# A hybrid decoder layer's norms over the model width: operands in PSUM, transposes in pairs, half of the chunks scaled on VectorE

## The chip, the cores and the metric

The kernel runs on one NeuronCore of a Trainium2 chip. The metric is the device time of one execution in microseconds (us); lower is better. The engines are named as in the profile: PE is TensorE (matrix multiply; PEld is its weight load), DVE is VectorE, ACT is ScalarE, POOL is GpSimd, SP is SyncE, whose queue issues the loads. SBUF is the on-chip memory that all engines read, PSUM the accumulation memory that PE writes and that DVE and ACT read and write.

## The reference

One decoder layer over 256 tokens of width 2048, all in float32: a SwiGLU feed-forward half step, a mixer (attention beside a convolution), and a second half step, each followed by a layer norm over the model width.

```python
x = layer_norm(ALPHA * x + 0.5 * swiglu_ffn(x, w_gate1, w_up1, w_down1), ln1_g, ln1_b)
u = x @ w_in + b_in
mixed = concat([attention(q, k, v, sinks), conv_group(conv_in)]) @ w_out + b_out
x = layer_norm(ALPHA * x + mixed, ln2_g, ln2_b)
x = layer_norm(ALPHA * x + 0.5 * swiglu_ffn(x, w_gate2, w_up2, w_down2), ln3_g, ln3_b)
```

Here `layer_norm(x, g, b)` is `(x - mean) * rsqrt(var + eps) * g + b` along the 2048 columns. The first two norms (`ln1`, `ln2`) are the ones that the change touches.

## The kernel before

**Products.** Each float32 product is made of three products of split operands: an operand is a high part (rounded to a reduced format, by a copy on ACT) and a low part (the rest, by a subtraction on DVE or POOL). A weight unit of 128 x 1024 is thus loaded, copied to `hi` by ACT (L126) and subtracted to `lo` by DVE or, for the units listed in `pooled`, by POOL (L128). `POOL_FIRST` lists the units just behind each of the two norms whose subtraction POOL does: 0, 1, 2 and 4. Units are called u0, u1, ... below, counted from the norm.

**Two token blocks.** The 256 tokens are two blocks b = 0 and 1 of 128 partitions. The product ahead of a norm (`tokens_by`) sums into one PSUM tile `acc` per block and per 512 columns. Its last six weight units are held back for block 1 (`SKEW`): PE ends block 0 first, and while it does the six held steps of block 1 (six matmuls each), the other engines turn block 0 into the operand of the next product. When a block's last sum is done, DVE evacuates it (L265), takes the statistics (L268, L320) and the inverse root (`rsqrt`, one column wide, L278 to L288). All of this stands in DVE's queue in the order in which the code emits it.

**From tokens to features** (`norm_to_features`, once per block and norm). The 2048 columns are four chunks c = 0 to 3 of 512. DVE makes `z = (x - mean) * r` for all four (L325). PE turns each chunk by four transposes into a PSUM tile `tp` (L302); a tile holds two chunks, and there are two such tiles (`psA`, tag `gu`). ACT applies gain and bias, which lie along partitions after the transpose, in four pieces of 128 x 128, from PSUM into `z` in SBUF (L310), then copies the chunk to the high half of `xcat` (L311); DVE subtracts for the low half (L312).

**The order.** Nothing is scheduled by the compiler: each engine runs its instructions in the order of emission. `Steps` counts steps; `LN_AT` is a table of (step after the call, chunk, action), action 0 being the transposes, 1 the scaling, 2 the low half. Before the change block 0's transposes of chunk 0 come after the fourth held step, and those of chunks 1, 2 and 3 after the fifth. The next product (`token_group`, tile `grp`) starts after the sixth; its step t needs chunk t // 2 of `xcat` and unit ut, six steps for block 0, then six for block 1, then the last two for both. Block 1's transposes stand between block 0's steps of this product.

**Waits.** An instruction that needs another engine's result waits on a semaphore; one that needs an earlier result of its own engine does so too. The order listings below show these waits by engine (`Activation_49` is ACT, `DVE_49` DVE, `PE_49` PE, `DMAHW` a load).

Of the kernel before, what the change touches and what calls it, by code (L numbers as in the profile page):

```python
# [9 lines left out]
F32 = mybir.dt.float32  # L10
# [3 lines left out]
AF = mybir.ActivationFunctionType  # L14
ALU = mybir.AluOpType
# [3 lines left out]
P = 128  # L19
# [24 lines left out]
CAP = 4.0  # L44
CONV_AT = (1, 3, 1)
HB = 5
POOL_FIRST = (0, 1, 2, 4)
POOL_SPAN = (20, 84)
POOL_SHARE = (4, 7)
ZB = 5  # L50

LN_AT = ((5, 0, 0), (5, 0, 1), (6, 1, 0), (6, 2, 0), (6, 1, 1), (6, 3, 0), (6, 0, 2), (6, 2, 1), (7, 3, 1), (7, 0, 2), (7, 0, 2), (8, 0, 2))
ATT = (1, 1, 2, 2, 4, 6, 7)
ENGINES = {getattr(mybir.EngineType, e) for e in ("PE", "DVE", "Activation", "Pool", "SP")}

# [125 lines left out]
def hybrid_layer(  # L181
# [3 lines left out]
    nc = tc.nc  # L185
# [7 lines left out]
    psC = ctx.enter_context(tc.tile_pool(name="psC", bufs=1, space=PSUM))  # L193
# [25 lines left out]
    for n in (first, second):  # L219
        pooled |= {n + i for i in POOL_FIRST}  # L220
    st = Steps(nc, wpool, items, sources, pooled, xT, xcat)
# [9 lines left out]
    for lo_, base, mult, step in ((0, 0, 1, -1), (P, -1, -1, 1), (2 * P, 0, 1, -1)):  # L231
        nc.gpsimd.affine_select(
            out=mask[:, lo_ : lo_ + P], in_=mask[:, lo_ : lo_ + P], compare_op=ALU.is_ge,
            fill=NEG, base=base, pattern=[[step, P]], channel_multiplier=mult,
        )
    bias = const.tile([P, 26], F32, name="bias")
# [4 lines left out]
    xt = act.tile([P, 2, D], F32, name="xt")  # L241
# [31 lines left out]
    def rsqrt(var, y, between=()):  # L273

        v = small.tile([P, 1], F32, tag="rs_v", name="rs_v")
        w = small.tile([P, 1], F32, tag="rs_w", name="rs_w")
        t = small.tile([P, 1], F32, tag="rs_t", name="rs_t")
        nc.vector.tensor_scalar(out=v, in0=var, scalar1=EPS, scalar2=None, op0=ALU.add)  # L278
        nc.vector.tensor_scalar(
            out=y.bitcast(I32), in0=v.bitcast(I32), scalar1=-0.5, scalar2=RSQRT_SEED,  # L280
            op0=ALU.mult, op1=ALU.add,
        )
        nc.vector.tensor_scalar(out=w, in0=v, scalar1=-0.5, scalar2=None, op0=ALU.mult)
        for _ in range(3):
            if between:
                between.pop(0)()
            nc.vector.tensor_scalar(out=t, in0=y, scalar1=y, scalar2=w, op0=ALU.mult, op1=ALU.mult)
            nc.vector.tensor_scalar(out=y, in0=t, scalar1=1.5, scalar2=y, op0=ALU.add, op1=ALU.mult)  # L288
# [3 lines left out]
    def norm_to_features(b, stats, par, gcol, xc):  # L292

        mv, r = par[:, b, 0:2], par[:, b, 2:3]
        zs, tps = [], []

        def turn(c):
            if c % 2 == 0:
                tps.append(psA.tile([P, 2, 4, P], F32, tag="gu", name=f"tp{b}_{c}"))
            tp = tps[c // 2][:, c % 2]  # L300
            for k in range(4):
                nc.tensor.transpose(tp[:, k], zs[c][:, k * P : (k + 1) * P], ident)  # L302

        def scale(c):
            tp = tps[c // 2][:, c % 2]
            k4, cols = slice(4 * c, 4 * c + 4), slice(b * P, (b + 1) * P)
            full = zs[c].rearrange("p (k n) -> p k n", k=4)
            for k in range(4):
                g, be = (lnp[:, gcol + n, 4 * c + k : 4 * c + k + 1] for n in range(2))
                nc.scalar.activation(full[:, k], tp[:, k], AF.Identity, scale=g, bias=be)  # L310
            nc.scalar.copy(xc[:, k4, 0, cols], full)  # L311
            waiting.append(lambda: nc.vector.tensor_tensor(  # L312
                out=xc[:, k4, 1, cols], in0=full, in1=xc[:, k4, 0, cols].bitcast(F32), op=ALU.subtract
            ))

        def settle(most=9):
            for _ in range(min(most, len(waiting))):
                waiting.pop(0)()

        nc.vector.bn_aggr(out=mv, in_=stats[b].rearrange("p c s -> p (c s)"))  # L320
        rsqrt(mv[:, 1:2], r, waiting)
        settle()
        for c in range(NC_):
            z = act.tile([P, 512], F32, tag="z", name=f"z{b}_{c}", bufs=ZB)
            nc.vector.tensor_scalar(  # L325
                out=z, in0=xt[:, b, c * 512 : (c + 1) * 512], scalar1=mv[:, 0:1], scalar2=r,
                op0=ALU.subtract, op1=ALU.mult,
            )
            zs.append(z)
        for n, c, what in LN_AT:  # L330
            st.at(n, lambda c=c, what=what: (turn(c) if what == 0 else scale(c) if what == 1 else settle(1)))

    def residuals(par, row, more, eng, start, every):

# [210 lines left out]
    x1 = act.tile([P, KT, 2, S], F32R, tag="xcat", name="xcat1")  # L545
    par1, par2, par3 = params("par1"), params("par2"), params("par3")
    ffn(xcat, "1", 0, begun1, lambda pool: None, lambda b, s: norm_to_features(b, s, par1, 0, x1))


# [355 lines left out]
```

## Time and profile before

| | before |
|---|---|
| device time, three runs | 1789.01, 1789.95, 1790.3 us (median 1789.95) |
| the profiled execution | 1786.97 us |
| its span, first to last instruction | 1785.2 us |
| mean granted TensorE clock | 0.997 |
| DVE busy | 1058.7 us (59%) |
| ACT busy | 837.8 us (47%) |
| POOL busy | 142.2 us (8%) |
| bytes read from HBM | 332.86 MB, 188 GB/s over the span |

The profile is of one execution, whose own time is 1786.97 us; the span leaves out 1.8 us ahead of the first and behind the last instruction. The times of its rows are microseconds from the start of the span. A row of the timeline gives start, length, engine, line, operation, output <- input, their sizes, a count of merged instructions, and in brackets how long the engine had been idle and what ended the wait. The first norm lies at 731 to 770 us, the second at 1024 to 1063 us.

### The profile page before, as it was taken

Reading aid. Unit: us, or ns where it says so; the run is one execution under the profiler, and the core shown is the slowest. Engines: PE = TensorE matmul, PEld = TensorE weight load, DVE = VectorE, ACT = ScalarE, POOL = GpSimd, SP = SyncE. Lnnn points to the kernel's source line nnn. Section 1 sums busy time; section 2 is a strip of 40 time slices with the busy share of each in tenths; the row PEclk is TensorE's granted clock in tenths of the full one; section 3 lists DMA queues with packets and bytes.
Section 4 is the critical chain, followed back from the end, with each engine's and each line's share of the span. In section 5 each row is a group of like instructions: output and inputs, shape, how many; then the busy total and the mean of one; then the engine's idle time right before and its main releaser. Section 6 shows DMA issues by size and latency. Waiting matters only on the chain.

```text
span 1785.2 us, 23510 instructions
## 1 busy us (share of the span) xinstructions
PE 1750.2 (98%) x9550; PEld 1510.2 (85%) x9550; DVE 1058.7 (59%) x1386; ACT 837.8 (47%) x1145; POOL 142.2 (8%) x82
## 2 busy tenths in 40 slices
PE   8999999999999999999998999999999999999997
PEld 7888888888888888789997778888888888888885
DVE  6555555445555555658889676855544455555546
ACT  6544444334444443575653574544443334444431
POOL 0000000000000000205654420000000000000000
PEclk9999999999999999999999999999999999999999
DMA  9655555554555555445534445555555555555651
GB/s 334 236 189 189 189 189 189 193 200 175 188 189 189 189 210 190 148 163 179 179 142 165 165 165 200 215 189 189 187 201 189 193 200 189 188 188 189 223 209 48
DMA packets 52092, 336.48 MB, mean 188 GB/s; under 512 B 6288, under 2 KB 6416, under 8 KB 13072
## 3 DMA queue, kind: packets, MB, share of 16 engines
q1 hardware_dynamic: 51984, 334.98, 51.6%
q8 instruction: 75, 1.23, 0.3%
q14 instruction: 33, 0.27, 0.0%
HBM read 332.86 MB, written 2.10 MB: 188 GB/s over the span
## 4 chain that ended last, share of the span: by engine, by line
PE 95%; DVE 3%; ACT 1%; DMA 0%; issue 0%; SPq 0%; DVEq 0%
PE gu L491 35%; PE gu L497 18%; PE acc L384 10%; PE acc L386 10%; PE acc L385 10%; PE in_c L384 2%; PE in_c L385 2%; PE in_c L386 2%; PE grp L386 1%; PE grp L385 1%; PE grp L384 1%; PE in_q L384 1%; DVE z L325 1%; PE in_q L385 1%; PE in_q L386 1%; DVE conv L649 0%
## 5 line engine op out<-in xcount | busy, mean ns | idle before, releaser
L128 DVE TENSOR_TENSOR lo<-raw,hi 128x1024 fp32r<-128x1024 f32 (+1 forms) x569 | 701.9, 1240 | 234.7 <-ACT hi L126 233.6
L126 ACT CAST hi<-raw 128x1024 fp32r<-128x1024 f32 (+1 forms) x614 | 640.5, 1048 | 348.8 <-PE acc L386 319.6
L491 PE MATMUL gu<-xcat,hi 128*128 128x512 f32 x2688 | 673.1, 392 | 0.0
L491 PEld LDWEIGHTS gu<-xcat,hi 128*128 128x128 f32 x2688 | 483.7, 189 | 86.6
L497 PEld LDWEIGHTS gu<-xcat,lo 128*128 128x128 f32 x2688 | 366.7, 190 | 26.2
L497 PE MATMUL gu<-xcat,lo 128*128 128x256 f32 x2688 | 374.8, 282 | 0.0
L511 DVE TENSOR_TENSOR both<-gu,corr 128x512 f32<-128x512 f32 x84 | 58.1, 692 | 382.4 <-ACT corr L510 382.4
L384 PE MATMUL acc<-hi,hh 128*128 128x512 f32 x704 | 274.1, 389 | 0.0
L385 PE MATMUL acc<-lo,hh 128*128 128x512 f32 x704 | 273.9, 389 | 0.0
L386 PE MATMUL acc<-hi,hl 128*128 128x512 f32 x704 | 273.9, 389 | 0.0
L510 ACT COPY corr<-gu 128x512 f32<-128x512 f32 x84 | 49.2, 586 | 415.6 <-PE gu L497 415.6
L128 POOL TENSOR_TENSOR lo<-raw,hi 128x1024 fp32r<-128x1024 f32 x45 | 112.2, 2501 | 810.7 <-ACT hi L126 810.6
L386 PEld LDWEIGHTS acc<-hi,hl 128*128 128x128 f32 x704 | 132.2, 188 | 27.4
L384 PEld LDWEIGHTS acc<-hi,hh 128*128 128x128 f32 x704 | 132.2, 188 | 27.3
L385 PEld LDWEIGHTS acc<-lo,hh 128*128 128x128 f32 x704 | 132.2, 188 | 27.1
L649 DVE SCALAR_TENSOR_TENSOR conv<-hc,cw_sb,conv 128x256 f32<-128x256 f32 x232 | 93.5, 481 | 3.3 <-ACT conv L645 3.3
L384 PE MATMUL in_c<-xcat,hi 128*128 128x256 f32 x256 | 73.9, 289 | 0.0
L386 PE MATMUL in_c<-xcat,lo 128*128 128x256 f32 x256 | 72.4, 283 | 0.0
L385 PE MATMUL in_c<-xcat,hi 128*128 128x256 f32 x256 | 72.4, 283 | 0.0
L265 DVE SCALAR_TENSOR_TENSOR xt<-acc,xt 128x512 f32<-128x512 f32 x48 | 32.9, 689 | 55.9 <-PE acc L386 55.9
L384 PE MATMUL acc<-hi,mh 128*128 128x512 f32 x128 | 51.1, 399 | 7.0 <-DVE xt L265 4.6
L384 PEld LDWEIGHTS in_c<-xcat,hi 128*128 128x128 f32 x256 | 49.0, 191 | 2.4 <-issue 2.3
(125 smaller groups left out, 1121.9 us busy)
## 6 DMA issues: line engine op xcount, KB each, us to landing
raw<-in_wu SPq DMA_DIRECT2D x168, 1024.0 KB, 4.8
raw<-in_wd SPq DMA_DIRECT2D x88, 1024.0 KB, 4.7
raw<-in_win SPq DMA_DIRECT2D x26, 1024.0 KB, 4.8
raw<-in_wout SPq DMA_DIRECT2D x16, 1024.0 KB, 4.7
raw<-in_wt SPq DMA_DIRECT2D x4, 1024.0 KB, 4.7
raw<-in_wt SPq DMA_DIRECT2D x6, 512.0 KB, 6.5
xt<-in_x SPq DMA_DIRECT2D x2, 1024.0 KB, 7.7
rg<-in_rows SPq DMA_DIRECT2D x8, 256.0 KB, 5.1
```

Source lines behind the costliest of these rows:

```text
L126: nc.scalar.copy(hi, raw)
L128: eng.tensor_tensor(out=lo, in0=raw, in1=hi.bitcast(F32), op=ALU.subtract)
L265: nc.vector.scalar_tensor_tensor(out=y, in0=ps, scalar=factor, in1=y, op0=ALU.mult, op1=ALU.add)
L325: nc.vector.tensor_scalar(out=z, in0=xt[:, b, c * 512 : (c + 1) * 512], scalar1=mv[:, 0:1], scalar2=r, op0=ALU.subtract, op1=ALU.mult,)
L384: nc.tensor.matmul(ps, s_hi, m_hi, start=start, stop=False)
L385: nc.tensor.matmul(ps, s_hi, m_lo, start=False, stop=False)
L386: nc.tensor.matmul(ps, s_lo, m_hi, start=False, stop=stop)
L491: nc.tensor.matmul(gu[:, m, :], hi[:, q * P : (q + 1) * P], xc[:, k].rearrange("p a n -> p (a n)"), start=k == 0, stop=False,)
L497: nc.tensor.matmul(gu[:, m, S:], lo[:, q * P : (q + 1) * P], xc[:, k, 0, :], start=False, stop=k == KT - 1,)
L510: nc.scalar.copy(corr, gu[:, :, S:])
L511: nc.vector.tensor_tensor(out=both, in0=gu[:, :, :S], in1=corr, op=ALU.add)
L649: nc.vector.scalar_tensor_tensor(out=acc if k < CK - 1 else cv[:, i], in0=hc[:, k : k + S], scalar=cw_sb[:, i, k : k + 1], in1=acc, op0=AL ...
```

## The change

Five things change, all at the two norms:

- `z` is made by an instruction with two tensor inputs (L339 of the changed kernel): the second is `r`, copied to one column of a PSUM tile `rp` (L336) and read for every column.
- Gain and bias are applied in place in the PSUM tile `tp`: chunks 0 and 1 by ACT (L314), chunks 2 and 3 by DVE (L316), each in four pieces of 128 x 128.
- The high half is copied and the low half subtracted from `tp` in PSUM (L323, L324), no longer from `z` in SBUF.
- In `LN_AT` the transposes come in pairs: chunks 0 and 1 after the third held step (step 4 of the table), 2 and 3 after the fourth. Action 2 is now the high half and 3 the low half.
- POOL takes the subtraction of u3 as well.

```diff
-POOL_FIRST = (0, 1, 2, 4)
+POOL_FIRST = (0, 1, 2, 3, 4)
-LN_AT = ((5, 0, 0), (5, 0, 1), (6, 1, 0), (6, 2, 0), (6, 1, 1), (6, 3, 0), (6, 0, 2), (6, 2, 1), (7, 3, 1), (7, 0, 2), (7, 0, 2), (8, 0, 2))
+LN_AT = (
+    (4, 0, 0), (4, 1, 0), (4, 0, 1), (4, 0, 2), (5, 2, 0), (5, 3, 0), (5, 1, 1), (5, 1, 2), (5, 0, 3), (5, 2, 1),
+    (5, 3, 1), (6, 1, 3), (6, 2, 2), (6, 3, 2), (6, 2, 3), (7, 3, 3),
+)
...
+        rp = psC.tile([P, 1], F32, tag="conv", name=f"rp{b}")
...
         def scale(c):
             tp = tps[c // 2][:, c % 2]
-            k4, cols = slice(4 * c, 4 * c + 4), slice(b * P, (b + 1) * P)
-            full = zs[c].rearrange("p (k n) -> p k n", k=4)
             for k in range(4):
                 g, be = (lnp[:, gcol + n, 4 * c + k : 4 * c + k + 1] for n in range(2))
-                nc.scalar.activation(full[:, k], tp[:, k], AF.Identity, scale=g, bias=be)
-            nc.scalar.copy(xc[:, k4, 0, cols], full)
+                if c < 2:
+                    nc.scalar.activation(tp[:, k], tp[:, k], AF.Identity, scale=g, bias=be)
+                else:
+                    nc.vector.tensor_scalar(
+                        out=tp[:, k], in0=tp[:, k], scalar1=g, scalar2=be, op0=ALU.mult, op1=ALU.add
+                    )
+
+        def high(c):
+            tp = tps[c // 2][:, c % 2]
+            k4, cols = slice(4 * c, 4 * c + 4), slice(b * P, (b + 1) * P)
+            nc.scalar.copy(xc[:, k4, 0, cols], tp)
             waiting.append(lambda: nc.vector.tensor_tensor(
-                out=xc[:, k4, 1, cols], in0=full, in1=xc[:, k4, 0, cols].bitcast(F32), op=ALU.subtract
+                out=xc[:, k4, 1, cols], in0=tp, in1=xc[:, k4, 0, cols].bitcast(F32), op=ALU.subtract
             ))
...
+        nc.vector.tensor_copy(rp, r)
         for c in range(NC_):
             z = act.tile([P, 512], F32, tag="z", name=f"z{b}_{c}", bufs=ZB)
-            nc.vector.tensor_scalar(
-                out=z, in0=xt[:, b, c * 512 : (c + 1) * 512], scalar1=mv[:, 0:1], scalar2=r,
+            nc.vector.scalar_tensor_tensor(
+                out=z, in0=xt[:, b, c * 512 : (c + 1) * 512], scalar=mv[:, 0:1], in1=rp.to_broadcast([P, 512]),
                 op0=ALU.subtract, op1=ALU.mult,
             )
```

DVE's queue at the first norm, from block 0's `z` on, before the change (`lo_5876` is the low part of u3, `acc_5693` the last sum of block 1, `par` holds mean and inverse root):

```order
L325 TENSOR_SCALAR z_0_5819<-xt,par_119 128x512 [waits DVE_49]
L325 TENSOR_SCALAR z_1_5821<-xt,par_119 128x512
L325 TENSOR_SCALAR z_2_5823<-xt,par_119 128x512
L325 TENSOR_SCALAR z_3_5825<-xt,par_119 128x512
L128 TENSOR_TENSOR lo_5876<-raw_5710,hi_5875 128x1024 [waits DMAHW7_49,PE_49,Activation_49]
L312 TENSOR_TENSOR xcat_118<-z_0_5819,xcat_118 128x4x128 [waits DVE_49]
L265 SCALAR_TENSOR_TENSOR xt<-acc_5693,xt 128x512 [waits PE_49]
L268 BN_STATS st_5161<-xt 128x6 [waits DVE_49]
```

The same place in the changed kernel (`tp_0` holds the turned chunks 0 and 1, `tp_2` chunks 2 and 3; `lnp` gain and bias):

```order
L336 COPY rp_5806<-par_119 128x1 [waits DVE_49]
L339 SCALAR_TENSOR_TENSOR z_0_5821<-xt,par_119,rp_5806 128x512 [waits DVE_49]
L339 SCALAR_TENSOR_TENSOR z_1_5823<-xt,par_119,rp_5806 128x512
L339 SCALAR_TENSOR_TENSOR z_2_5825<-xt,par_119,rp_5806 128x512
L339 SCALAR_TENSOR_TENSOR z_3_5827<-xt,par_119,rp_5806 128x512
L324 TENSOR_TENSOR xcat_118<-tp_0_5857,xcat_118 128x4x128 [waits Activation_49]
L316 TENSOR_SCALAR tp_2_5881<-tp_2_5881,lnp 128x128 [waits PE_49]
L316 TENSOR_SCALAR tp_2_5881<-tp_2_5881,lnp 128x128 [waits DVE_49] x7
L324 TENSOR_TENSOR xcat_118<-tp_0_5857,xcat_118 128x4x128
L324 TENSOR_TENSOR xcat_118<-tp_2_5881,xcat_118 128x4x128 [waits DVE_49,Activation_49]
L268 SCALAR_TENSOR_TENSOR xt<-acc_5693,xt 128x512 [waits PE_49]
L271 BN_STATS st_5161<-xt 128x6 [waits DVE_49]
```

Ahead of block 1's evacuation there now stand eight scalings, each waiting for the one before it, and three low halves instead of one. The second low half (of chunk 1) waits for nothing: the wait of the first (of chunk 0) is for ACT's copy of chunk 1, because all accesses to one PSUM tile are kept in order of emission.

ACT's queue at the same place before the change (`hi_5875` is u3):

```order
L310 ACTIVATE z_0_5819<-tp_0_5865,lnp 128x128 [waits DVE_49,PE_49]
L310 ACTIVATE z_0_5819<-tp_0_5865,lnp 128x128 x3
L311 CAST xcat_118<-z_0_5819 128x4x128 [waits Activation_49]
L126 CAST hi_5875<-raw_5710 128x1024
L310 ACTIVATE z_1_5821<-tp_0_5865,lnp 128x128 [waits DVE_49,PE_49]
L310 ACTIVATE z_1_5821<-tp_0_5865,lnp 128x128 x3
L311 CAST xcat_118<-z_1_5821 128x4x128 [waits Activation_49]
```

And in the changed kernel (`hi_5871` is u2, `hi_5904` u3):

```order
L314 ACTIVATE tp_0_5857<-tp_0_5857,lnp 128x128 [waits PE_49]
L314 ACTIVATE tp_0_5857<-tp_0_5857,lnp 128x128 [waits Activation_49] x3
L323 CAST xcat_118<-tp_0_5857 128x4x128 [waits Activation_49]
L129 CAST hi_5871<-raw_5710 128x1024 [waits DMAHW7_49,DVE_49]
L314 ACTIVATE tp_0_5857<-tp_0_5857,lnp 128x128 [waits Activation_49] x4
L323 CAST xcat_118<-tp_0_5857 128x4x128 [waits Activation_49]
L129 CAST hi_5904<-raw_5710 128x1024 [waits DVE_49,PE_49]
L323 CAST xcat_118<-tp_2_5881 128x4x128 [waits DVE_49]
L323 CAST xcat_118<-tp_2_5881 128x4x128
```

The scalings of one tile wait for each other, the first also for the last transpose of chunk 1; u2's copy, which stood ahead of the first scaling, now stands between the two chunks, and the copies of chunks 2 and 3 wait for DVE's eighth scaling. On PE only the transposes move: eight after the third held step, eight after the fourth, and for block 1 eight behind step t = 2 and eight behind t = 3 of the next product.

More of the change, by code (lines that the diff above doesn't have):

```diff
@@ L330, in norm_to_features @@
         for n, c, what in LN_AT:
-            st.at(n, lambda c=c, what=what: (turn(c) if what == 0 else scale(c) if what == 1 else settle(1)))
+            st.at(n, lambda c=c, what=what: (turn, scale, high, lambda c: settle(1))[what](c))
     def residuals(par, row, more, eng, start, every):
```

## The prediction, made before the changed kernel was run

> **What bounds the kernel now.** I read the page first: shares, the chain that ended last, the costliest groups.
>
> ```profile
> PE 1750.2 (98%) x9550; PEld 1510.2 (85%) x9550; DVE 1058.7 (59%) x1386; ACT 837.8 (47%) x1145; POOL 142.2 (8%) x82
> ...
> PE 95%; DVE 3%; ACT 1%; DMA 0%; issue 0%; SPq 0%; DVEq 0%
> ```
>
> PE is the bound: it is busy for 98% of the span and 95% of the chain. An edit elsewhere can only bring what PE waits, so the view of PE's waits comes next (total, times, longest).
>
> ```profile
> PE tp L302 <- DVE z L325: 4.7, 4, 1.9
> PE grp L386 <- DVE xcat L312: 3.0, 3, 1.6
> ```
>
> Both are the norms': 7.7 us in two norms, 0.4% of the time. PE's timeline at the first norm shows where (the number in brackets is the wait):
>
> ```profile
> 731.00 0.39 PE L384 MATMUL acc<-hi,hh 128*128 128x512 f32 x1
> ...
> 736.53 0.63 PE L302 MATMUL tp<-ident,z 128*128 128x128 f32 x4
> 739.06 0.63 PE L302 MATMUL tp<-ident,z 128*128 128x128 f32 x4 [0.51 <-DVE z L325]
> 741.56 1.06 PE L302 MATMUL tp<-ident,z 128*128 128x128 f32 x8 [1.87 <-DVE z L325]
> 748.83 0.50 PE L386 MATMUL grp<-hi,xcat 128*128 128x512 f32 x1 [1.64 <-DVE xcat L312]
> 753.70 1.53 PE L302 MATMUL tp<-ident,z 128*128 128x128 f32 x12 [0.20 <-ACT z L310]
> ```
>
> From 731.00 to 736.53 PE runs the 24 matmuls of four held steps, 0.227 us each; four transposes take 0.53. After the last transposes (755.23) stand 42 matmuls of the first product's block steps, to 764.76. DVE and POOL say why z is late:
>
> ```profile
> 731.20 0.69 DVE L265 SCALAR_TENSOR_TENSOR xt<-acc,xt 128x512 f32<-128x512 f32 x1 [5.85 <-PE acc L386]
> ...
> 733.69 7.43 POOL L128 TENSOR_TENSOR lo<-raw,hi 128x1024 fp32r<-128x1024 f32 x3 [694.48 <-ACT hi L126]
> ...
> 735.07 6.80 DVE L325 TENSOR_SCALAR z<-xt,par 128x512 f32<-128x512 f32 x4
> ...
> 744.05 0.69 DVE L265 SCALAR_TENSOR_TENSOR xt<-acc,xt 128x512 f32<-128x512 f32 x1 [0.45 <-PE acc L386]
> ...
> 750.84 1.92 DVE L325 TENSOR_SCALAR z<-xt,par 128x512 f32<-128x512 f32 x4
> ```
>
> Four z take 6.80 us beside POOL's three subtractions and 1.92 us without them: the two engines exclude each other. From the evacuation to the first z are 3.87 us. At the second norm the same rows stand 292.97 and 292.94 us later:
>
> ```profile
> 1024.17 0.69 DVE L265 SCALAR_TENSOR_TENSOR xt<-acc,xt 128x512 f32<-128x512 f32 x1 [4.02 <-PE acc L386]
> 1046.64 1.53 PE L302 MATMUL tp<-ident,z 128*128 128x128 f32 x12 [0.23 <-ACT z L310]
> ```
>
> so one working does for both.
>
> **What the pieces cost.** Groups by form (count, busy, mean ns) and ACT's timeline:
>
> ```profile
> L649 DVE SCALAR_TENSOR_TENSOR conv<-hc,cw_sb,conv 128x256 f32<-128x256 f32 x232 | 93.5, 481 | 3.3 <-ACT conv L645 3.3
> L782 DVE TENSOR_SCALAR cv<-tk,cmv,cr 128x512 f32<-128x512 f32 x4 | 3.1, 806 | 0.1
> L511 DVE TENSOR_TENSOR both<-gu,corr 128x512 f32<-128x512 f32 x84 | 58.1, 692 | 382.4 <-ACT corr L510 382.4
> L466 DVE TENSOR_TENSOR ht<-slt,grp 128x256 f32<-128x256 f32 x4 | 1.6, 418 | 1.0 <-ACT slt L464 1.0
> ...
> L287 DVE TENSOR_SCALAR rs_t<-par,rs_w 128x1 f32<-128x1 f32 x6 | 1.6, 271 | 0.1
> ...
> L310 ACT ACTIVATE z<-tp,lnp 128x128 f32<-128x128 f32 x64 | 24.1, 456 | 9.2 <-PE tp L302 9.0
> L645 ACT ACTIVATE conv<-hc,cp_sb,cw_sb 128x256 f32<-128x256 f32 x8 | 4.3, 575 | 0.0
> L697 ACT ACTIVATE pr<-sc,nm 128x128 f32<-128x128 f32 x16 | 5.9, 367 | 8.3 <-DVE nm L688 8.2
> ...
> 737.19 1.51 ACT L310 ACTIVATE z<-tp,lnp 128x128 f32<-128x128 f32 x4 [0.86 <-PE tp L302]
> 738.73 0.62 ACT L311 CAST xcat<-z 128x512 fp32r<-128x512 f32 x1
> 739.26 1.04 ACT L126 CAST hi<-raw 128x1024 fp32r<-128x1024 f32 x1
> ```
>
> - **Columns on DVE**: 692 less 418 is 274 ns for 256 columns, 137 for 128.
> - **The new z** reads SBUF and PSUM with one pointer operand, as L649 does at 256 columns (481 ns, all 232 of them beside POOL's work of that stage): 0.755 us. Neighbours overlap: L325's 1.92 for four of 0.54 puts starts 0.46 apart, 0.08 less than the length, so 0.67 here. The z lose POOL's 6.80 but are slower than the free 1.92.
> - **DVE's scaling** of 128 columns in PSUM has two pointers, as L782 at 512: 806 - 3 x 137 = 395 ns; L287, one column with two pointers, gives 271 + 137 = 408. I take 0.40. Without any pointer L511 gives 692 - 411 = 0.28, the low end; L649's whole 0.48, in place, is the high end.
> - **ACT's scaling** now writes PSUM. L310 has it to SBUF at 0.456; low end L697's 0.367 (one pointer), high end L645's 0.575 (to PSUM, 256 columns). I take 0.456, the same operation and size.
> - **A wait for the own engine**: ACT's four scalings end at 738.70 and the copy starts at 738.73: 0.03 us, and the overlap of neighbours is lost. Four chained scalings on ACT take 4 x 0.486 = 1.94 instead of 1.51; eight on DVE 8 x 0.43 = 3.44.
> - **The copy of r**: at most L287's 0.27, taken as 0.2.
>
> **The changed norm, step by step**, on the clock of the first norm; the two kernels are alike up to 735.07.
>
> 1. z of block 0: starts 735.27; z0 done 736.03, z1 736.70, all by 738.04 instead of 741.87.
> 2. PE is through three held steps at 735.15, waits 0.9 for z0 and 0.1 for z1; chunk 1 is turned at 737.40 (0.63 after its start). Then 6 matmuls, 8 transposes (1.06) and 12 matmuls: block 1's sum is done at 742.43, where before it was at 744.05. So far 1.6 us are won.
> 3. ACT's first scaling waits for both chunks of its tile (737.43): scalings 1.94, copy 0.62, u2's weight copy 1.04 (0.1 of it under its neighbours), scalings 1.94, copy 0.62: done at 743.40.
> 4. DVE's first low half waits for that last copy, though chunk 0's own was done at 739.99. Behind it are queued the eight scalings, two more low halves **and block 1's evacuation**. The low half takes 0.6, the scalings 3.44: 747.47.
> 5. ACT copies chunks 2 and 3 (0.52 + 0.62), to 748.64; DVE's low half of chunk 2 follows, and block 1 is evacuated from 749.27: 5.2 us later than before, 6.8 after its sum was done.
> 6. Block 1's first z starts 3.87 later, plus 0.6 for the fourth low half in between and 0.2 for r: 753.94; z0 done 754.70, z1 755.37.
> 7. PE meanwhile waits 1.3 us for chunk 0's low half (step t = 0), 1.25 for chunk 1's (t = 2, 748.1), reaches block 1's transposes at 749.04 and waits **5.7 us** for z0. Both chunks are turned at 756.04.
> 8. Block 1 repeats 3 and 4 without the weight copy: ACT 5.2 us (761.24), DVE low half 0.6, scalings 3.44, low half of chunk 1 0.69: about 765.9. PE waits for it in block 1's t = 2.
> 9. From there 22 of the 36 matmuls are left, 4.99 us: 770.9 against 764.76. **Plus 6.1 us a norm, 12.2 in both.**
>
> **The clock.** The longest wait of today's PE outside the start is followed by this:
>
> ```profile
> 947.53 0.47 PE L384 MATMUL acc<-hi,mh 128*128 128x512 f32 x1 [4.63 <-DVE xt L265]
> 947.84 0.55 PE L385 MATMUL acc<-lo,mh 128*128 128x512 f32 x1
> 948.19 0.63 PE L386 MATMUL acc<-hi,ml 128*128 128x512 f32 x1
> 948.61 0.63 PE L384 MATMUL acc<-hi,mh 128*128 128x512 f32 x1
> ...
> 951.17 0.47 PE L384 MATMUL acc<-hi,mh 128*128 128x512 f32 x1
> ```
>
> After 4.63 us of idling the matmuls come 0.43 apart for 3.6 us; after 1.87 (741.56) eight transposes still take 1.06. A wait of 5.7 should do the same. Eight transposes at half speed cost 1.06 more, less the 0.1 of waiting between them; later matmuls lose what they would have waited in step 8. **Plus 0.9 a norm, 1.8.**
>
> **What is covered.** No edit moves a DMA, so SP's queue keeps its order. u3's subtraction leaves DVE (1.2 us) while DVE idles in step 4 anyway; POOL has it done by 747, needed for t = 3 after 755. u4 and u5 are copied by ACT at 749 to 751, needed for t = 4 after 758. u6 follows block 1's last copy (about 766.5), its low part by 769.2; PE takes it at 770.9. If that cover went, a late unit would cost up to 1.7 us.
>
> **Sum**: 14.0 us over the profiled execution's 1786.97, so 1801.0; the median of the runs lies 2.98 higher, which makes **1804**. The scalings carry the doubt: 16 of ACT's and 16 of DVE's lie on a norm's path, so 0.1 us on each is 6.4 us. Low ends of both: 2 x 16 x (0.089 + 0.12) = 6.7 less. High ends: 2 x 16 x (0.119 + 0.08) = 6.4 more.
>
> **Rivals.**
>
> - *The clock holds*: 1802.2. For it: only one wait of this length is in the trace.
> - *Short scalings*, at their low ends: 1797.3. Against it: L782 and L287 agree on what two pointers cost.
> - *No change*: with both scalings some 0.2 us shorter still (0.20 and 0.25) the sum is 14.0 - 13.0, so 1791. Nothing in the trace is that short with two pointers. [...]
> - *Faster*: block 1's evacuation finds DVE free. It would start at 742.43, z0 would be ready at 747.86, PE would wait 1.4 there and nowhere after, and end at 762.4: 2.4 us won a norm, 1785.2. It decides at step 5: the way from chunk 1's transpose to the evacuation would have to take 5.0 us; the rows make it 11.8. The gains of steps 1 and 2 speak for it, the order of DVE's queue against it.
>
> **Chances.** Forecast 0.55, clock holds 0.2, short scalings 0.14, high end (1810) 0.04, no change 0.04, faster 0.03. The range 1796 to 1809 holds the first three. About 0.2% is what a measurement here can tell from no change: faster 0.03, within 0.04, slower 0.93.
>
> **What would show it.** In the changed profile: four z in about 2.8 us beside POOL (step 1); chunk 0's low half on DVE starting right behind chunk 1's copy on ACT (4); the eight scalings 0.43 apart (4); block 1's evacuation some 7 us behind its last matmul (5); a wait of 5 to 6 us of PE for z, once a norm (7), with slow matmuls behind it; PE's second wait for chunk 1's low half in block 1 (8). It is wrong if scalings run under 0.3 us apart, or if block 1's evacuation starts before 745.

## The result, and the profile after

| | before | after |
|---|---|---|
| device time, five runs each | 1789.01 us (1787.54 to 1790.3) | 1803.25 us (1801.43 to 1803.93) |
| ratio, 95% interval | | 1.0077 (1.0065 to 1.0088) |
| the profiled execution / its span | 1786.97 / 1785.2 us | 1802.97 / 1801.2 us |
| mean granted clock | 0.997 | 0.991 |

The changed kernel is slower by 14.24 us. The page and PE's waits of the changed kernel (total, times, longest):

```profile
PE 1756.8 (98%) x9550; PEld 1515.6 (84%) x9550; DVE 1059.2 (59%) x1420; ACT 827.0 (46%) x1113; POOL 145.2 (8%) x84
...
PE tp L306 <- DVE z L339: 12.2, 4, 5.2
PE grp L398 <- ACT hi L129: 5.7, 1, 5.7
PE grp L400 <- DVE xcat L324: 5.4, 5, 1.1
```

PE's two waits on the norms, 7.7 us in all before, are 17.6 now (12.2 + 5.4). PE is also "busy" for 6.6 us longer with the same 9550 matmuls: some of them run slower. PE's timeline at the first norm:

```profile
737.22 1.22 PE L306 MATMUL tp<-ident,z 128*128 128x128 f32 x8 [0.92 <-DVE z L339]
...
744.98 0.50 PE L400 MATMUL grp<-hi,xcat 128*128 128x512 f32 x1 [1.08 <-DVE xcat L324]
...
749.09 0.50 PE L400 MATMUL grp<-hi,xcat 128*128 128x512 f32 x1 [1.07 <-DVE xcat L324]
...
755.52 1.97 PE L306 MATMUL tp<-ident,z 128*128 128x128 f32 x8 [5.23 <-DVE z L339]
757.14 0.78 PE L398 MATMUL grp<-hi,xcat 128*128 128x512 f32 x1
...
767.32 0.50 PE L400 MATMUL grp<-hi,xcat 128*128 128x512 f32 x1 [1.09 <-DVE xcat L324]
...
777.65 0.39 PE L400 MATMUL grp<-hi,xcat 128*128 128x512 f32 x1
```

The early waits of 0.51 and 1.87 us for z have become one of 0.92, and in their place stands one of 5.23 for block 1's z, with eight transposes at 1.97 us behind it. DVE at the same place shows why z is late:

```profile
732.26 0.69 DVE L268 SCALAR_TENSOR_TENSOR xt<-acc,xt 128x512 f32<-128x512 f32 x1 [5.85 <-PE acc L400]
...
736.13 0.16 DVE L336 COPY rp<-par 128x1 f32<-128x1 f32 x1
736.33 2.72 DVE L339 SCALAR_TENSOR_TENSOR z<-xt,par,rp 128x512 f32<-128x512 f32 x4
744.24 0.69 DVE L324 TENSOR_TENSOR xcat<-tp,xcat 128x512 fp32r<-128x512 f32 x1 [5.19 <-ACT xcat L323]
744.85 3.60 DVE L316 TENSOR_SCALAR tp<-tp,lnp 128x128 f32<-128x128 f32 x8
...
750.19 0.68 DVE L268 SCALAR_TENSOR_TENSOR xt<-acc,xt 128x512 f32<-128x512 f32 x1
...
754.71 2.72 DVE L339 SCALAR_TENSOR_TENSOR z<-xt,par,rp 128x512 f32<-128x512 f32 x4
```

Four z take 2.72 us instead of 6.80. Then DVE stands idle for 5.19 us, and low halves and scalings follow in front of block 1's evacuation at 750.19. What DVE waits for is on ACT:

```profile
738.48 1.82 ACT L314 ACTIVATE tp<-tp,lnp 128x128 f32<-128x128 f32 x4 [2.44 <-PE tp L306]
740.33 0.59 ACT L323 CAST xcat<-tp 128x512 fp32r<-128x512 f32 x1
...
743.62 0.59 ACT L323 CAST xcat<-tp 128x512 fp32r<-128x512 f32 x1
```

Chunk 0's own copy ends at 740.92; the low half starts at 744.24, with the end of chunk 1's copy (744.21).

**Where the 16.0 us between the two profiled executions lie.** The span is cut at block 0's evacuation and at the last `grp` matmul of each norm:

| stretch | before | after | difference |
|---|---|---|---|
| to the evacuation of block 0, first norm | 731.20 | 732.26 | +1.06 |
| first norm (to the last `grp` matmul) | 38.62 | 45.39 | +6.77 |
| mixer | 254.35 | 255.76 | +1.41 |
| second norm | 38.62 | 45.39 | +6.77 |
| to the last matmul | 709.08 | 709.08 | 0.00 |

The norms hold 13.54 us. The first row is code that does not differ (731.59 to 732.62 in the nine other kernels below). Nor does the mixer's code; its row is explained under "the clock" below.

### The profile page after: what moved, and what is told of

The parts are those of the page before. It is cut to its first block, busy times and chain, and to the rows that moved or that the text cites. A ratio compares the mean times of both kernels' runs of the same rounds, so it can differ in the third digit from the quotient of the medians.

```text
span 1801.2 us, 23497 instructions
## 1 busy us (share of the span) xinstructions
PE 1756.8 (98%) x9550; PEld 1515.6 (84%) x9550; DVE 1059.2 (59%) x1420; ACT 827.0 (46%) x1113; POOL 145.2 (8%) x84
## 4 chain that ended last, share of the span: by engine, by line
PE 94%; DVE 4%; ACT 1%; DMA 0%; issue 0%; SPq 0%; DVEq 0%; ACTq 0%
PE gu L505 34%; PE gu L511 18%; PE acc L398 10%; PE acc L400 10%; PE acc L399 10%; PE in_c L398 2%; PE in_c L399 2%; PE in_c L400 2%; PE grp L400 1%; PE grp L399 1%; PE grp L398 1%; PE in_q L398 1%; PE in_q L399 1%; PE in_q L400 1%; ACT tp L314 1%; DVE tp L316 1%
## 5 line engine op out<-in xcount | busy, mean ns | idle before, releaser
L400 PE MATMUL acc<-hi,ml 128*128 128x512 f32 x128 | 51.2, 400 | 0.0
```

Of the source, the lines that this page charges most:

```text
L400: nc.tensor.matmul(ps, s_lo, m_hi, start=False, stop=stop)
```

## Experiments

Three kernels start from the changed one, six from the kernel before. "Norms" are the two stretches of the table above, from each profile. The kernel before was timed anew with each of the three series of experiments (medians 1789.09, 1789.76 and 1789.08 us), and each ratio is to the median of its own series; "z and u3" belongs to the first series, u3 alone and the three kernels built on "z and u3" to the second, and the moved table entry to the third.

| kernel | device time | ratio to before (95%) | norms |
|---|---|---|---|
| changed | 1803.25 | 1.0077 (1.0065 to 1.0088) | 45.39, 45.39 |
| changed, scaling into SBUF | 1795.42 | 1.0037 (1.0024 to 1.0051) | 42.39, 42.50 |
| changed, PE kept busy in the wait | 1800.45 | 1.0064 (1.0051 to 1.0076) | 44.72, 44.73 |
| changed, low half of chunk 0 first | 1795.20 | 1.0033 (1.0021 to 1.0045) | 41.66, 42.15 |
| before + new z | 1786.98 | 0.9992 (0.9983 to 1.0001) | 37.51, 37.49 |
| before + u3 on POOL | 1794.89 | 1.0025 (1.0014 to 1.0036) | 41.06, 41.08 |
| before + both ("z and u3") | 1781.22 | 0.9957 (0.9945 to 0.9970) | 34.68, 34.65 |
| z and u3 + in place | 1790.57 | 1.0004 (0.9995 to 1.0013) | 38.90, 38.88 |
| z and u3 + half on VectorE | 1796.74 | 1.0044 (1.0031 to 1.0056) | 43.05, 43.10 |
| z and u3 + changed order | 1800.44 | 1.0064 (1.0051 to 1.0078) | 44.66, 45.34 |

### Which parts gain: z alone, u3 alone, both

The new z alone, put into the kernel before:

```diff
+        rp = psC.tile([P, 1], F32, tag="conv", name=f"rp{b}")
...
+        nc.vector.tensor_copy(rp, r)
...
-            nc.vector.tensor_scalar(
-                out=z, in0=xt[:, b, c * 512 : (c + 1) * 512], scalar1=mv[:, 0:1], scalar2=r,
+            nc.vector.scalar_tensor_tensor(
+                out=z, in0=xt[:, b, c * 512 : (c + 1) * 512], scalar=mv[:, 0:1], in1=rp.to_broadcast([P, 512]),
```

> The kernel before with one part of the change: r copied to a PSUM column and z made by scalar_tensor_tensor from it; scaling, order and unit 3 as before. Theory (z's 6.80 us beside GpSimd becomes about 2.8, and the first transposes come 0.3 us later for the copy and the longer single operation): PE's waits for z of 0.51 and 1.87 us in each norm go, but unit 3's low half and the low half of 2.65 us stay in front of block 1's evacuation, so about 1 us per norm is left of it: -2 us in all, ratio 0.999. Rival (the new form of z is itself a cost of the change): slower than before by 1 to 3 us, ratio 1.001.

Measured 0.9992; the norms lose 2.2 us. The theory's size held, though in the timed runs the gain can't be told from none. PE's waits for z in that kernel (total, times, longest) show why it is so little:

```profile
PE tp L303 <- DVE z L327: 4.9, 2, 2.5
```

The waits of 0.51 and 1.87 us are gone, but in each norm PE now waits 2.5 us for block 1's z instead. Next, u3 alone:

```diff
-POOL_FIRST = (0, 1, 2, 4)
+POOL_FIRST = (0, 1, 2, 3, 4)
```

> The kernel before with one part of the change: unit 3 of the next weights subtracted by GpSimd. Theory (z as tensor_scalar from SBUF stops for each of GpSimd's subtractions of 2.4 us, and there is one more of them beside z or the low halves): block 1's evacuation or its z comes later by up to one subtraction in each norm, +3 to +4 us in all, ratio 1.002; so unit 3 pays only together with the new z. Rival (VectorE is rid of 1.2 us in any case): -1 to -3 us, ratio 0.999.

Measured 1.0025, slower as the theory had it, and by 5.1 us rather than 3 to 4. DVE's z and then PE's timeline of that kernel:

```profile
736.48 8.83 DVE L325 TENSOR_SCALAR z<-xt,par 128x512 f32<-128x512 f32 x4
```

```profile
742.97 0.63 PE L302 MATMUL tp<-ident,z 128*128 128x128 f32 x4 [1.87 <-DVE z L325]
745.37 1.11 PE L302 MATMUL tp<-ident,z 128*128 128x128 f32 x4 [1.77 <-DVE z L325]
746.14 0.78 PE L384 MATMUL acc<-hi,hh 128*128 128x512 f32 x1
```

The four z now stop for a fourth subtraction of POOL (8.83 us against 6.80), PE waits three times within 6 us (0.50 ahead of these two), and matmuls 0.43 us apart follow. The theory had no such slow matmuls; whether they are the surplus, no run shows. Both edits together:

> The kernel before with two parts of the change: z from the PSUM column and unit 3 of the next weights subtracted by GpSimd instead of VectorE; scaling into SBUF by ScalarE and the order as before. Theory (these two parts are gains, and what makes the changed kernel slower is the rest): z no longer stops for GpSimd, so GpSimd may run beside it, VectorE is rid of 1.2 us ahead of block 1's evacuation, and of the 7.7 us that PE waits in the two norms nearly all goes: -7 to -8 us, ratio 0.996. Rival (GpSimd's third subtraction then only meets the low halves, of which one took 2.65 us beside it): -2 us as with z alone, ratio 0.999.

Measured 0.9957, the theory's value. The two effects do not add up: -2.1 and +5.1 by themselves, -7.9 together (each against before in its own series). VectorE's rows of the first norm:

```profile
736.46 2.73 DVE L327 SCALAR_TENSOR_TENSOR z<-xt,par,rp 128x512 f32<-128x512 f32 x4
740.48 2.08 DVE L313 TENSOR_TENSOR xcat<-z,xcat 128x512 fp32r<-128x512 f32 x1 [1.29 <-ACT xcat L312]
742.79 0.69 DVE L265 SCALAR_TENSOR_TENSOR xt<-acc,xt 128x512 f32<-128x512 f32 x1 [0.23 <-PE acc L388]
```

and PE's waits there in both norms:

```profile
PE tp L303 <- ACT z L311: 1.0, 4, 0.3
PE tp L303 <- DVE z L327: 0.8, 2, 0.4
```

z with one operand in PSUM runs at its full speed beside POOL (2.73 us for four here, and 2.72 for block 1's four in the changed kernel, where POOL is idle), so POOL may take u3. Block 1's evacuation comes 10.39 us after block 0's, as soon as its sum is done: VectorE had been idle for 0.23 us. 1.8 us of waiting are left of 8.1 (7.7, and 0.4 for ACT's scaling). Two of the change's five parts are thus worth -7.9 us, and this kernel is faster than both the kernel before and the changed one. No run has the new instruction with r in SBUF, so whether the operation or the place of r frees it from POOL is not told apart by the runs.

Beside POOL's subtractions the rows differ by instruction: the z that reads SBUF and PSUM is not slowed (2.73 us against 2.72), the low half from two SBUF tensors is (2.08 us against 0.68), and so is the z of the kernel before (6.80 us against 1.92), which reads one tensor and two single columns, all in SBUF. That "the two engines exclude each other" holds for these two, not for the new z; why, no run shows.

### Which parts cost: one of the other three at a time, on "z and u3"

In place in PSUM, all four chunks by ACT:

```diff
-            full = zs[c].rearrange("p (k n) -> p k n", k=4)
+            full = tp
```

> The kernel with z from PSUM and unit 3 on GpSimd (1781.2), with ScalarE's scaling of all four chunks now in place in PSUM and the halves read from there; order as before. Theory (in place, a tile's operations wait for each other): ScalarE's scaling waits for the pair's other chunk, each scaling for the one ahead of it, the low half of chunk 0 for the copy of chunk 1, so block 1's evacuation is 2 to 4 us later in each norm: about 1790, ratio 1.0005. Rival (in place is no cost where one engine does all the scaling): 1781 to 1782, ratio 0.996.

Measured 1.0004, that is +9.4 us over "z and u3" by the medians (8.7 when each is held against before in its own series, 8.5 in the norms). The theory's size is right; its place is so only in part. VectorE waits for chunk 1's copy here too:

```profile
744.00 0.69 DVE L313 TENSOR_TENSOR xcat<-tp,xcat 128x512 fp32r<-128x512 f32 x1 [4.85 <-ACT xcat L312]
```

The low half itself reads PSUM and takes 0.69 instead of 2.08 us, not stopped by POOL, whose fourth subtraction ends at 744.30; the wait ahead of it went from 1.29 to 4.85. Block 1's evacuation comes 12.25 us after block 0's, only 1.9 later than in "z and u3", and PE waits just 0.34 us for block 1's z. Most of the cost is on PE itself: a transpose into the second half of a tile now waits until ACT has scaled and copied the first half, where it had waited for the scaling alone (0.20 us in the kernel before).

```profile
740.74 1.53 PE L303 MATMUL tp<-ident,z 128*128 128x128 f32 x12 [1.13 <-ACT xcat L312]
754.19 1.53 PE L303 MATMUL tp<-ident,z 128*128 128x128 f32 x12 [1.75 <-ACT xcat L312]
```

These waits are 5.8 us in both norms, and those for low halves another 2.5. Half of the scaling on VectorE, into SBUF:

```diff
-                nc.scalar.activation(full[:, k], tp[:, k], AF.Identity, scale=g, bias=be)
+                if c < 2:
+                    nc.scalar.activation(full[:, k], tp[:, k], AF.Identity, scale=g, bias=be)
+                else:
+                    nc.vector.tensor_scalar(
+                        out=full[:, k], in0=tp[:, k], scalar1=g, scalar2=be, op0=ALU.mult, op1=ALU.add
+                    )
```

> The kernel with z from PSUM and unit 3 on GpSimd (1781.2), with chunks 2 and 3 scaled by VectorE into SBUF; order as before. Theory (eight scalings, 2.64 us where they wrote SBUF, stand in VectorE's queue ahead of block 1's evacuation or its z): that evacuation and z are later by 3 us and more in each norm and the waits for z come back: about 1795, ratio 1.003. Rival (ScalarE's 6 us of scaling were the limit, and sharing them helps or costs nothing): 1779 to 1783, ratio 0.995.

Measured 1.0044, +15.5 us (14.9 against before in its own series): the size was right, the mechanism only half. Block 1's evacuation is hardly later (743.12, 11.36 after block 0's, against 10.39). It is chunk 3's scaling that is late, behind block 1's z in VectorE's queue; VectorE first, then PE:

```profile
750.04 2.72 DVE L332 SCALAR_TENSOR_TENSOR z<-xt,par,rp 128x512 f32<-128x512 f32 x4
752.68 1.36 DVE L314 TENSOR_SCALAR z<-tp,lnp 128x128 f32<-128x128 f32 x4
```

```profile
747.83 0.69 PE L393 MATMUL grp<-hi,xcat 128*128 128x512 f32 x1 [2.51 <-DVE xcat L318]
...
757.09 1.09 PE L303 MATMUL tp<-ident,z 128*128 128x128 f32 x8 [3.29 <-ACT z L312]
```

ACT's queue stands behind that scaling as well (its copy of chunk 3 waits 9.27 us for it), so block 1's scalings on ACT come late and PE waits 3.29 us for the tile. The wait of 2.51 us ahead of it is for chunk 1's low half, which reads SBUF and takes 2.60 us beside POOL's subtraction of u4 (0.68 in "z and u3"). Last, the changed order, with the high half as an action of its own and all scaling by ACT into SBUF:

```diff
-LN_AT = ((5, 0, 0), (5, 0, 1), (6, 1, 0), (6, 2, 0), (6, 1, 1), (6, 3, 0), (6, 0, 2), (6, 2, 1), (7, 3, 1), (7, 0, 2), (7, 0, 2), (8, 0, 2))
+LN_AT = (
+    (4, 0, 0), (4, 1, 0), (4, 0, 1), (4, 0, 2), (5, 2, 0), (5, 3, 0), (5, 1, 1), (5, 1, 2), (5, 0, 3), (5, 2, 1),
+    (5, 3, 1), (6, 1, 3), (6, 2, 2), (6, 3, 2), (6, 2, 3), (7, 3, 3),
+)
```

> The kernel with z from PSUM and unit 3 on GpSimd (1781.2), with the changed order (transposes in pairs from the fourth step on, high and low halves as steps of their own); all scaling by ScalarE into SBUF. Theory (all transposes, scalings and low halves of a block then stand in one stretch ahead of block 1's evacuation, where before's order lets that evacuation pass three of the low halves): four low halves in front of it, each with up to 2.4 us of GpSimd's subtraction beside it, make it 4 to 6 us late and the wait for z comes back: 1792 to 1798, ratio 1.003 to 1.005. Rival (earlier transposes only bring everything forward): 1779 to 1782, ratio 0.995.

Measured 1.0064, +19.2 us (18.6 against before in its own series), more than expected. VectorE's rows say where:

```profile
747.40 2.42 DVE L325 TENSOR_TENSOR xcat<-z,xcat 128x512 fp32r<-128x512 f32 x1 [3.32 <-ACT xcat L324]
749.75 0.68 DVE L268 SCALAR_TENSOR_TENSOR xt<-acc,xt 128x512 f32<-128x512 f32 x1
```

Block 1's evacuation stands behind chunk 2's low half, that waits 3.32 us for ACT, which in this order scales chunks 2 and 3 (2.90 us) and casts a weight unit before it copies chunk 2. The evacuation comes 18.03 us after block 0's; PE waits 8.19 us for z. Each of the three parts alone undoes the gain. They don't add up either: 9.4 + 15.5 + 19.2 us is 44, all three together cost 22.0 (1803.25 less 1781.22). They lengthen the same way from block 0's transposes to block 1's, though each at another place of it.

### What holds up the changed kernel

Scaling into SBUF, all else as changed:

```diff
+            full = zs[c].rearrange("p (k n) -> p k n", k=4)
...
-                    nc.scalar.activation(tp[:, k], tp[:, k], AF.Identity, scale=g, bias=be)
+                    nc.scalar.activation(full[:, k], tp[:, k], AF.Identity, scale=g, bias=be)
...
-                        out=tp[:, k], in0=tp[:, k], scalar1=g, scalar2=be, op0=ALU.mult, op1=ALU.add
+                        out=full[:, k], in0=tp[:, k], scalar1=g, scalar2=be, op0=ALU.mult, op1=ALU.add
...
         def high(c):
-            tp = tps[c // 2][:, c % 2]
+            tp = zs[c].rearrange("p (k n) -> p k n", k=4)
```

> The changed kernel, with the scaled chunks written to z's place in SBUF instead of in place in PSUM; engines, order and unit 3 as changed. Theory (in place, operations of one tile wait for each other: the low half of chunk 0 waits for the copy of chunk 1, 3.3 us, and the copies of chunks 2 and 3 for the eighth scaling): the low halves start when their own copy ends, block 1 is evacuated 3 to 4.5 us earlier in each norm, and 8 to 9 of the 13.5 us go: about 1794, ratio 1.002 to 1.003. Rival (the eight scalings on VectorE and the early pairs cost it by themselves, wherever they write): 1802 to 1804, ratio 1.007 to 1.008.

Measured 1.0037: 7.8 us less than the changed kernel, a little short of the theory; the norms lose 5.9 of their 13.5. VectorE in that kernel:

```profile
740.34 0.69 DVE L325 TENSOR_TENSOR xcat<-z,xcat 128x512 fp32r<-128x512 f32 x1 [1.62 <-ACT xcat L324]
740.95 2.64 DVE L317 TENSOR_SCALAR z<-tp,lnp 128x128 f32<-128x128 f32 x8
...
744.82 2.48 DVE L325 TENSOR_TENSOR xcat<-z,xcat 128x512 fp32r<-128x512 f32 x1 [0.52 <-ACT xcat L324]
747.23 0.68 DVE L268 SCALAR_TENSOR_TENSOR xt<-acc,xt 128x512 f32<-128x512 f32 x1
```

The first low half starts 3.6 us earlier after the z (an idle time of 1.62 instead of 5.19), and eight scalings take 2.64 instead of 3.60. But a low half that reads SBUF meets POOL again (2.48 us), so that the evacuation comes 2.6 us earlier (15.30 after block 0's, instead of 17.93), not 3 to 4.5. This edit changes two things, the waits and the length of the scalings. The next changes the waits alone: the same instructions, one table entry moved.

```diff
-    (4, 0, 0), (4, 1, 0), (4, 0, 1), (4, 0, 2), (5, 2, 0), (5, 3, 0), (5, 1, 1), (5, 1, 2), (5, 0, 3), (5, 2, 1),
+    (4, 0, 0), (4, 1, 0), (4, 0, 1), (4, 0, 2), (5, 2, 0), (5, 3, 0), (5, 0, 3), (5, 1, 1), (5, 1, 2), (5, 2, 1),
```

> The changed kernel with one entry of its order moved: the low half of chunk 0 is issued ahead of the scaling of chunk 1 instead of behind its copy; the same instructions, all in place in PSUM. Theory (what is in place waits by order within its tile, not by what it reads, and VectorE's 3.3 us of waiting for a copy of another chunk are what pushes block 1's evacuation back): the low half of chunk 0 runs at about 741 instead of 744.24, ScalarE's scaling of chunk 1 isn't delayed since the hi cast stands in between, VectorE's eight scalings begin at about 741.6, block 1's evacuation is about 3.3 us earlier in each norm, and with it 6 to 10 of the 13.5 us go, part of them clock: 1793 to 1797, ratio 1.002 to 1.005. Rival (the time lies in the scalings themselves, or ScalarE now waits for VectorE instead): 1802 to 1804, ratio 1.007 to 1.008.

Measured 1.0033, 8.05 us less than the changed kernel; the norms lose 7.0 of their 13.5. VectorE:

```profile
741.22 0.69 DVE L324 TENSOR_TENSOR xcat<-tp,xcat 128x512 fp32r<-128x512 f32 x1 [1.91 <-ACT xcat L323]
741.83 3.60 DVE L316 TENSOR_SCALAR tp<-tp,lnp 128x128 f32<-128x128 f32 x8
...
747.18 0.68 DVE L268 SCALAR_TENSOR_TENSOR xt<-acc,xt 128x512 f32<-128x512 f32 x1
```

The scalings are as long as before this edit (3.60 us), the wait is 1.91 instead of 5.19, and the evacuation comes 14.66 us after block 0's: 3.27 earlier. That wait was one of order, not of data, and it accounts for about half of the loss. Where the other half lies was not tried out in the changed kernel; the runs on "z and u3" show that each of the three parts by itself can cost as much.

### The clock

PE kept busy in the long wait: 36 transposes of the identity into the tile that block 1's own transposes then overwrite.

```diff
             tp = tps[c // 2][:, c % 2]
+            if b == 1 and c == 0:
+                for k in range(36):
+                    nc.tensor.transpose(tp[:, k % 4], ident, ident)
             for k in range(4):
```

> The changed kernel with 36 more transposes of the identity into the PSUM tile that block 1's transposes then overwrite, about 4.8 us of work at 0.13 us each in the wait of 5.2 us ahead of them; nothing else differs. Theory (about 1 us per norm is PE running at a lower granted clock after that wait): the eight transposes behind it take 1.2 and not 1.97 us, matmuls stay 0.23 us apart, and 1.5 to 2.5 us go: about 1801, ratio 1.0066. Rival (the slow stretch is only the pipeline filling, or is hidden by waits that follow): no change, 1803, ratio 1.0077.

Measured 1.0064, 2.8 us less than the changed kernel by the medians, though the intervals of the two ratios overlap. In the profiles each norm's stretch is 0.66 to 0.67 us shorter, which is what the clock costs there: less than the 1 us expected. The rest of the 2.8 was not traced. It may be the mixer's, which differs from one execution to the next: the profiled execution of the filled kernel is its slowest (1801.47, granted clock 0.995), and the other four have 0.997. The timeline of PE with the filling, then 15 us at each norm (stretch, its length, PE busy and its instructions, granted clock, DMA share, GB/s):

```profile
749.76 4.09 PE L307 MATMUL tp<-ident 128*128 128x128 f32 x36
755.15 1.31 PE L309 MATMUL tp<-ident,z 128*128 128x128 f32 x8 [1.31 <-DVE z L342]
```

```profile
750.00:765.00 15.00, 13.42 (x84) 1.00 0.33 126
1050.00:1065.00 15.00, 13.46 (x84) 1.00 0.34 129
```

The same stretches of the changed kernel itself, and two of its mixer:

```profile
750.00:765.00 15.00, 9.77 (x46) 0.77 0.37 140
950.00:965.00 15.00, 10.39 (x38) 0.77 0.55 200
990.00:1005.00 15.00, 12.68 (x55) 0.89 0.21 70
1050.00:1065.00 15.00, 9.55 (x38) 0.77 0.38 135
```

With the filling the clock stays at 1.00 and the eight transposes take 1.31 instead of 1.97. Those 0.66 us are all that is won: block 1's scalings on ACT start behind these transposes, and DVE's low halves behind the scalings. What the later matmuls gain is spent in waiting (0.27 us more for chunk 0's low half). The rows also explain the mixer's +1.41: the changed kernel has two slow stretches there (950 and 990), behind waits of 4.61 and 2.32 us. The kernel before has waits as long (4.63 and 2.33 us, its stretch 8 us earlier), but it has only half of the slow time behind the first and none behind the second:

```profile
940.00:955.00 15.00, 10.37 (x39) 0.89 0.58 211
980.00:1000.00 20.00, 17.40 (x84) 1.00 0.30 104
```

The same unchanged mixer took 254.1 to 254.4 us in seven of the eleven profiles compared here and 255.8 to 256.9 in the other four. "z and u3" is among the slower ones, with 256.93.

## Why the prediction was right

The forecast was 1804.0 us; 1803.25 was measured.

- **Step 1.** z: 2.72 us for four, beside POOL, against about 2.8; 743 ns each against 755; the copy of r 0.16 against 0.2.
- **Step 2.** PE's first wait 0.92 against 0.9.
- **Step 3.** ACT's four scalings 1.82 against 1.94, four in place at 431 ns each instead of 456.
- **Step 4.** The low half of chunk 0 does start with the end of chunk 1's copy. That this wait matters, the moved table entry shows (-8.05 us). DVE's eight scalings took 3.60 against 3.44, at 418 ns each.
- **Step 5.** Block 1's evacuation at 750.19, less the 1.06 of the start 749.13, against 749.27.
- **Steps 6 and 7.** Block 1's z at 754.71, so 753.65, against 753.94. PE's waits 1.08 and 1.07 against 1.3 and 1.25, the long one 5.23 against 5.7.
- **Steps 8 and 9.** The last wait of 1.09 for chunk 1's low half is there in the first norm. In the second it is not: the slow clock lasted until 1062 and used it up, as the prediction said for "later matmuls". There, too, the matmul starts as soon as that low half is done (1068.46, the low half ends at 1068.40), and so both norms take 45.39.
- **The clock.** Predicted 0.9 us a norm; the filled kernel shows 0.67, which is the eight transposes, as predicted. Without it a norm costs 44.72 - 38.62 = 6.10 us, the 6.1 of the sum.

The sum for the norms was 14.0 and came out at 13.54. In a norm the clock cost 0.23 us less than predicted, ACT's four sets of scalings 0.48 less (4 x 0.12) and DVE's two sets 0.32 more (2 x 0.16): the sizes were off in both directions and cancelled in part, which is luck. The two profiled executions differ by 16.0 because their unchanged parts differ by 2.5. The difference of the medians is 14.24, where the forecast of 1804.0 started from the median of three runs, 1789.95. That the time itself was met within 1 us is partly luck too: that median moved by 0.94 with two more runs, and the unchanged mixer alone varies by more.

Of the rivals, "the clock holds" fell by the row at 755.52 and the granted clock of 0.77 at both norms, "short scalings" and "no change" by the 418 and 431 ns. "Faster" needed 5.0 us from chunk 1's transposes to the evacuation. In the changed kernel it took 11.75 (738.44 to 750.19). The order of the low half (3.3 us, by the moved table entry) and DVE's scalings (3.60 us) closed that way about equally, and none of the kernels in the changed order came near it: with the entry moved it is still 8.5. What made a gain possible was the part that the prediction had counted only as 1.6 us won by step 2: the new z together with POOL's u3.

One price of the prediction belongs to its place only: u3 on POOL "while DVE idles in step 4 anyway" was taken as nothing. No run took it out of the changed kernel, so that it is nothing there was not tried; in the kernel before the same edit costs 5.1 us, and with the new z it gains 5.8 (1786.98 to 1781.22).

## What to carry to other kernels

Look at what stands in an engine's queue ahead of the instruction that the bound engine will wait for next: three sensible edits (in place, shared between two engines, earlier) each put something that PE needed (a free half of a tile, block 1's scalings, block 1's evacuation) behind a wait and lost 9 to 19 us, though VectorE was busy for 59% of the changed kernel's span and ScalarE for 46%. In this program work in place in a shared PSUM tile was kept in order of emission, readers of one half behind writers and readers of the other, so emit the readers of one half before the writers of the other; one table entry was worth 8 us. And measure the parts of a change by themselves and in pairs: two parts of this one, kept without the rest, make the kernel 0.43% faster (interval 0.30% to 0.55%).

## What the runs showed of the hardware

- **The slow clock came in portions.** Over rows of 1 us, from 725 to 1085 us in the kernel before and the changed one, the granted clock falls to 0.50 and no lower, and matmuls come 0.43 us apart instead of 0.227. Added up over these rows, every slow stretch is within 0.02 us of 3.42 us (one in each kernel) or 6.84 us (three in the changed one): one or two times the same portion. The stretches of 15 us agree: in 0.77 lie 0.23 x 15 / 0.5 = 6.9 us of slow clock, in 0.89 3.3 us ("z and u3" has both in its mixer). It does not start with the wait: in the changed kernel PE stops at 750.29 and 1051.45, and the clock falls 1.2 and 3.8 us later, until 758.3 and 1062.1, while the waits end at 755.5 and 1056.7. So equal waits cost different amounts. 4.63 us brought one portion in the kernel before and 4.61 two in the changed one; 2.33 brought none and 2.32 one. What sets the length of a portion and the time of its start, no run shows.
- **Short waits were followed by slow clock, too.** With waits of 0.50, 1.87 and 1.77 us within 6 us the clock was 0.77 from 740 to 755 (u3 alone), 6.9 us of slow clock; with 0.51 and 1.87 it stayed at 1.00 through the first norm of the kernel before.
- **Work in place in PSUM cost VectorE the overlap of neighbours.** Eight scalings of 128 columns took 3.60 us in place in PSUM, each waiting for the one before, and 2.64 us from PSUM into SBUF. One by itself took 418 ns against 403: what differs is mostly the distance from start to start, 0.45 us against 0.32.
